# Layer 1's residual through VectorE block transposes and DRAM, and two groups' decay differences on ScalarE

## The chip, the cores and the metric

The kernel runs on one core of a Trainium2 chip. The metric is device time in microseconds (us), the median of several executions of the whole program. One more execution was taken with the hardware profiler; its times are the ones quoted from the profile.

## What is computed

Two layers work on 272 tokens (16 learned ones and 256 of the input) of width 2048, in float32. Layer 0 is linear attention beside stick-breaking attention. Layer 1, in which the change lies, is a Mamba-2 mixer (SSD). Each layer ends in `layer_norm(ALPHA * h + f(h))` with ALPHA = 4^(1/4). Cut to layer 1:

```python
proj = einsum('btd,de->bte', h, w_in)
z, xbc, dt_raw = split(proj)                    # 4096, 4096+2*1024, 64 columns
xbc = silu(causal_depthwise_conv(xbc, conv_w, conv_b))
xs, bs, cs = split(xbc)                         # 8 groups of 8 heads
dt = softplus(dt_raw + dt_bias)
a_cum = cumsum(dt * -exp(a_log))
l_mat = exp(where(causal, a_cum[t] - a_cum[s], -inf))   # the decay
y = einsum(l_mat * (cs . bs), xs * dt) + d_skip * xs    # the group's mixing
y = rms_norm_groups(y * silu(z), norm_w, 8)
h = layer_norm(ALPHA * h + y @ w_out, ln_g, ln_b)
```

## The kernel before

**Layout.** The hidden state is kept with channels on partitions: `hacc` is 16 tiles of 128 channels by 272 tokens. Layer 1's output is built the other way, with tokens on partitions: `acc` holds two tiles of 128 tokens by 2048 channels. The residual ALPHA·h has to come from the first form into the second, which is a transposition of 2048 x 256 numbers.

**Units.** The weights stream in as units of 1 MB (L144, on the queue of SyncE, SP; three buffers `raw`). ScalarE (ACT) rounds each half to `whi` (L159), VectorE (DVE) or GpSimd (POOL) forms the rest `wlo` (L160), and TensorE (PE) multiplies: three products per pair of tiles (L178 to L180), 48 matmuls per input unit of 128 output columns. Every float32 product is made so. A group of layer 1 has the input units B, C, four x and four z; from the second group on, output units (L494 to L496, then L503 adds into `acc`) come two groups behind their mixing. I write z1 and z2 for the second and third z unit of group 0.

**Side tasks.** All else runs as tasks that are stepped between the matmuls of the units. A scheduler with a model of the machine then sets the order on each engine, but no engine waits for another except by data, by a buffer that is not free yet, or because its instructions are in order.

**Layer 1's start (`first1`).** Six units (B, C, z0, x0, x1, x2 of group 0) are multiplied before the normalisation of layer 0 is applied. `fix` (L955 to L958) applies it to their results afterwards: a small copy, L956 and L957 on DVE, then ACT; L956 also frees the PSUM bank, of which the units share four. Meanwhile `normalize0` (L994 on DVE, L997 on ACT) normalises `hacc` itself. Then `xhi` (ACT, L981) and `xlo` (DVE, L982) are split from it, 16 pieces each, for all units that follow: the last x unit (x3), z1, z2 and so on.

**The residual (`residual1`).** 32 PE transposes (L1010) of 128 x 128 go into PSUM, and eight ACT copies (L1011) bring them to `acc`, multiplied by ALPHA.

**The decay.** `dt_path` forms dt and its cumulated sums, writes them to DRAM (edr, L1048) and transposes them with PE (L1055) into `est`. For each group `load_decay` reads edr back, broadcast to all partitions (ebc, L1092, 1664 KB), into the buffer that held `hacc`. `decay1` then forms, for each of the eight heads, min(ebc − est, 0) with two DVE instructions (L1125 with 256 columns, L1126 with 144), and an Exp on ACT for each two heads (L1128); after products with the causal part this is M, a single buffer.

**The mixing (`mix_ssd`).** PE multiplies M with x·dt (L1255, L1261), DVE adds the skip (L1265), POOL multiplies by the gate (L1266), ACT forms yh (L1268) and squares (L1271, L1274), POOL adds the squares up (L1275) into ysq, and PE sums them over the channels (L1281) for the group's RMS norm. The factor of that norm, `rstd1`, is applied when the output units' results are added to `acc`.

Of the kernel before, what the change touches and what calls it, by code (L numbers as in the profile page):

```python
# [6 lines left out]
F32 = mybir.dt.float32  # L7
F32R = mybir.dt.float32r
AF = mybir.ActivationFunctionType
# [79 lines left out]
class _Body:  # L89
# [413 lines left out]
            self.nc.vector.scalar_tensor_tensor(a, ps, r[:, t : t + 1], a, op0=ALU.mult, op1=ALU.add)  # L503

    def out1_unit(self, i, u, split_next):
        self.finish(*self.mixers[6 + u[1]])
        pst = [self.pj(), self.pj()]
        for h in range(2):
            split_next(h)
            for t in range(2):  # L510
                self.out1_half(pst[t], u[1], t, *self.parts[i, h], h)
                self.tick()
        for t in range(2):
            self.out1_add(pst[t], u[1], t, u[2])
# [428 lines left out]
    def first1(self):  # L943


        nc, lp = self.nc, self.lp
        act, vec = nc.scalar.activation, nc.vector
        b1 = len(L0)

        def fix(ps, n, t0, o=None):  # L950
            w = T - t0
            uv = lp.tile([P, 2], F32, tag="uv", name=self.nm("uv"), bufs=2)
            if o is None:
                o = lp.tile([P, T], F32, tag="yu", name=self.nm("fix"), bufs=2)
            vec.tensor_copy(uv[:n], ps[:n, w : w + 2])  # L955
            vec.scalar_tensor_tensor(o[:n, :w], mean[:n, t0:], uv[:n, 0:1], ps[:n, :w], op0=ALU.mult, op1=ALU.subtract)  # L956
            vec.tensor_tensor(o[:n, :w], o[:n, :w], self.rs_p[:n, t0:], op=ALU.mult)  # L957
            act(o[:n, :w], o[:n, :w], AF.Identity, bias=uv[:n, 1:2], scale=-1.0)  # L958
            return o

        scr = lp.tile([P, HPG, 400], F32, tag="M", name="dt_scr").rearrange("p a b -> p (a b)")
        mean = scr[:, 2048 + T : 2048 + 2 * T]
        act(mean, self.mean_p, AF.Copy)

        both = scr[:64, 2048 + 2 * T : 2048 + 2 * T + TG]
        act(both, self.ps_dt[64:128, :TG], AF.Copy)
        vec.tensor_tensor(both, both, self.ps_dt[:64, :TG], op=ALU.add)
        self.tasks["dt"] = self.push(self.dt_path(fix(both, 64, 0, scr[:, 2048 : 2048 + T]), scr))
        self.normed = False
        norm = self.push(self.normalize0())  # L970
        self.tasks["res"] = self.push(self.residual1(norm))
        for n, u in enumerate(L1[:NFIRST]):
            i = b1 + n
            self.load_unit(i + 2)
            ps = self.pj()
            t0 = {"z": NM, "C": C0}.get(u[2], 0)
            self.in_unit(ps[:, : TG - t0], i, t0, TG, lambda h: self.split_half(i + 1, h))
            self.post(u, fix(ps, P, t0))
        self.finish(norm)
        for k in range(KT):  # L980
            act(self.xhi[:, k, :T], self.hacc[:, k, :], AF.Copy)  # L981
            vec.tensor_tensor(self.xlo[:, k, :T], self.hacc[:, k, :], self.xhi[:, k, :T].bitcast(F32), op=ALU.subtract)  # L982
        self.normed = True
        self.last = [
            next(i for i in reversed(self.traced()) if i.engine == e)
            for e in (mybir.EngineType.Activation, mybir.EngineType.DVE)
        ]
# [12 lines left out]
    def residual1(self, norm):  # L1000

        nc = self.nc
        while not self.normed:
            yield
        for t in range(2):
            for c in range(4):
                ps = self.po()
                for k in range(4):
                    a = self.hacc[:, 4 * c + k, NM + t * P : NM + (t + 1) * P]
                    nc.tensor.transpose(ps[:, k * P : (k + 1) * P], a, self.ident)  # L1010
                nc.scalar.activation(self.acc[:, t, c * 512 : (c + 1) * 512], ps, AF.Copy, scale=ALPHA)  # L1011
                yield

    def dt_path(self, ps, scr):
# [72 lines left out]
            self.load_decay(g)  # L1087

    def load_decay(self, g):
        eb = self.hp.tile([P, HPG, 416], F32, tag="hacc", name=self.nm("ebc"))  # L1090
        src = self.edr[g * HPG : (g + 1) * HPG, :].rearrange("h c -> (h c)").partition_broadcast(P)
        self.nc.sync.dma_start(eb.rearrange("p h c -> p (h c)"), src)  # L1092
        self.cur["ebc", g] = eb
# [5 lines left out]
    def decay1(self, g):  # L1099
# [22 lines left out]
        eb = self.cur["ebc", g]  # L1122
        for h in range(HPG):
            gh = g * HPG + h
            vec.tensor_scalar(M[:, h, 0:256], eb[:, h, 0:256], self.est[:, 0, 0, gh : gh + 1], 0.0, op0=ALU.subtract, op1=ALU.min)  # L1125
            vec.tensor_scalar(M[:, h, 256:400], eb[:, h, 256:400], self.est[:, 0, 1, gh : gh + 1], 0.0, op0=ALU.subtract, op1=ALU.min)  # L1126
            if h % 2:
                act(M[:, h - 1 : h + 1, :], M[:, h - 1 : h + 1, :], AF.Exp)  # L1128
                yield
        mt = self.mt  # L1130
        e2 = self.est2[:, 0, g * HPG : (g + 1) * HPG].rearrange("p (h o) -> p h o", o=1).broadcast_to([16, HPG, 16])
# [104 lines left out]
    def mix_ssd(self, g):  # L1236
# [46 lines left out]
        tmp = lp.tile([P, 2], F32, tag="rt", name=self.nm("rt"))  # L1283
        r = lp.tile([P, 2], F32, tag="rr", name=self.nm("rr"), bufs=3)
        self.rstd1[g] = r
        vec.tensor_scalar(m, ps[:, 0:32:16], 1.0 / 512, RMS_EPS, op0=ALU.mult, op1=ALU.add)
        act(r, m, AF.Ln)
        act(r, r, AF.Exp, scale=-0.5)
        self.newton(r, m, tmp)
# [2 lines left out]
    def tail(self):  # L1292
# [51 lines left out]
        def moments(t):  # L1344
            v, r, _, _ = sc[t]
            vec.bn_aggr(mvs[t], sts[t])
            if t == 1:
                act(dm, nid, AF.Copy, scale=mvs[t][:, 0:1])
            vec.tensor_scalar(v, mvs[t][:, 1:2], LN_EPS, None, op0=ALU.add)
            act(r, v, AF.Ln)  # L1350
            act(r, r, AF.Exp, scale=-0.5)

# [126 lines left out]
```

## Time and profile before

| | |
|---|---|
| time, median of 3 runs | 1382.75 us (1382.08 to 1382.94) |
| span of the profiled execution | 1385.0 us |
| PE busy | 1374.1 us, 99% of the span |
| DVE busy | 1030.8 us, 74% |
| ACT busy | 768.3 us, 55% |
| POOL busy | 263.1 us, 19% |
| layer 1's 32 transposes on PE (L1010) | 710.8 to 733.0 us |
| group 0's decay differences on DVE | 769.3 to 774.1 us |
| the wait of PE for group 0's ysq | 804.4 to 806.4 us |

The span runs from the first to the last instruction of the one profiled execution; it lies 2.25 us above the median of the runs. In a timeline row the columns are the start, the time until the last of the row's instructions ends, engine, line and operation, the written tile and what it reads, the shape and the count; in brackets stands how long the engine was idle before, and who ended that. Matmuls overlap, so the distance from one start to the next is what one costs. Page rows of DMA give the count, the size of one and the median time from issue to landing.

### The profile page before, as it was taken

What the parts mean: (1) busy time and instruction counts of PE and PEld (TensorE: products, weight loads), DVE (VectorE), ACT (ScalarE), POOL (GpSimd) and SP (SyncE); (2) the same over time, 40 slices, a digit from 0 to 9 for tenths busy, and PEclk for the clock granted to TensorE, in tenths of its full rate; (3) what the DMA queues carried; (4) which work ended last, traced back from release to release, by engine and by line L of the source; (5) the groups of instructions that cost most, each with busy time, mean ns of one, the idle gap of its engine ahead of it and who ended that gap; (6) DMA issues with size and microseconds to landing.
All of it is one profiled execution on the core that took longest, in us unless ns stands there. A gap on an engine that the chain in (4) does not pass through costs nothing.

```text
span 1385.0 us, 26232 instructions
## 1 busy us (share of the span) xinstructions
PE 1374.1 (99%) x10643; PEld 1323.9 (96%) x10643; DVE 1030.8 (74%) x1762; ACT 768.3 (55%) x1141; POOL 263.1 (19%) x253
## 2 busy tenths in 40 slices
PE   9999999999999999999999999999999999999998
PEld 8999999999999999999999999899898999989986
DVE  7858576576565674568899999787877778867687
ACT  6646455355345544556587667656565655656551
POOL 0000100100101100004401143331322323133221
PEclk9999999999999999999999999999999999999999
DMA  9656446546455545554355655465555555455561
GB/s 329 209 172 201 163 163 206 169 155 227 153 173 171 169 161 191 172 165 161 123 183 197 231 181 205 169 244 182 209 177 195 190 191 222 169 198 183 181 214 61
DMA packets 61945, 256.73 MB, mean 185 GB/s; under 512 B 26176, under 2 KB 29056, under 8 KB 33408
## 3 DMA queue, kind: packets, MB, share of 16 engines
q1 hardware_dynamic: 61104, 254.27, 53.3%
q8 instruction: 83, 1.36, 0.4%
q10 hardware_dynamic: 720, 0.79, 0.2%
q14 instruction: 38, 0.31, 0.1%
HBM read 249.29 MB, written 5.74 MB: 184 GB/s over the span
## 4 chain that ended last, share of the span: by engine, by line
PE 94%; DVE 4%; DMA 1%; issue 1%; POOL 0%; ACT 0%; SPq 0%; ACTq 0%; DVEq 0%; POOLq 0%
PE pj L179 25%; PE pj L178 25%; PE pj L180 25%; PE pj L494 4%; PE pj L496 4%; PE pj L495 4%; PE po L1255 1%; PE po L631 1%; DVE wlo L160 1%; PE po L1193 0%; DMA raw<-in_wts 0%; DVE M L1125 0%; PE z L1143 0%; DVE xt L1070 0%; DVE acc L503 0%
## 5 line engine op out<-in xcount | busy, mean ns | idle before, releaser
L178 PE MATMUL pj<-xhi,whi 128*128 128x272 f32 (+4 forms) x2560 | 732.1, 286 | 1.7 <-ACT xhi L330 0.8
L179 PE MATMUL pj<-xlo,whi 128*128 128x272 f32 (+4 forms) x2560 | 730.8, 286 | 0.0
L180 PE MATMUL pj<-xhi,wlo 128*128 128x272 f32 (+4 forms) x2560 | 730.1, 286 | 0.0
L159 ACT ACTIVATE whi<-raw 128x1024 fp32r<-128x1024 f32 (+2 forms) x434 | 449.2, 1039 | 398.3 <-PE pj L179 326.3
L160 DVE TENSOR_TENSOR wlo<-raw,whi 128x1024 fp32r<-128x1024 f32 (+2 forms) x405 | 503.4, 1247 | 209.6 <-ACT whi L159 199.6
L178 PEld LDWEIGHTS pj<-xhi,whi 128*128 128x128 f32 x2560 | 482.6, 189 | 4.3 <-ACT whi L159 1.1
L179 PEld LDWEIGHTS pj<-xlo,whi 128*128 128x128 f32 x2560 | 482.6, 189 | 1.2 <-issue 0.6
L180 PEld LDWEIGHTS pj<-xhi,wlo 128*128 128x128 f32 x2560 | 482.6, 189 | 0.8 <-issue 0.8
L178 PE MATMUL pj<-mixh,whi 128*128 128x272 f32 x384 | 111.0, 290 | 0.0
L180 PE MATMUL pj<-mixh,wlo 128*128 128x272 f32 x384 | 110.7, 289 | 0.0
L179 PE MATMUL pj<-mixl,whi 128*128 128x272 f32 x384 | 110.7, 288 | 0.0
L160 POOL TENSOR_TENSOR wlo<-raw,whi 128x1024 fp32r<-128x1024 f32 x29 | 73.1, 2520 | 193.7 <-ACT whi L159 193.7
L494 PE MATMUL pj<-whi,yh 128*128 128x512 f32 (+1 forms) x240 | 93.3, 389 | 0.0
L495 PE MATMUL pj<-wlo,yh 128*128 128x512 f32 (+1 forms) x240 | 92.6, 386 | 0.0
L496 PE MATMUL pj<-whi,yl 128*128 128x512 f32 (+1 forms) x240 | 92.2, 386 | 0.0
L261 POOL TENSOR_TENSOR gr<-gr,gsc 128x1088 f32<-128x1088 f32 x6 | 15.4, 2574 | 303.6 <-ACT gsc L260 303.6
L179 PEld LDWEIGHTS pj<-mixl,whi 128*128 128x128 f32 x384 | 72.4, 188 | 0.2
L180 PEld LDWEIGHTS pj<-mixh,wlo 128*128 128x128 f32 x384 | 72.3, 188 | 0.0
L178 PEld LDWEIGHTS pj<-mixh,whi 128*128 128x128 f32 x384 | 72.2, 188 | 0.2
L503 DVE SCALAR_TENSOR_TENSOR acc<-pj,rr,acc 128x512 f32<-128x512 f32 (+1 forms) x65 | 46.5, 733 | 13.9 <-PE pj L496 13.9
L496 PEld LDWEIGHTS pj<-whi,yl 128*128 128x128 f32 x240 | 45.1, 188 | 9.2
L494 PEld LDWEIGHTS pj<-whi,yh 128*128 128x128 f32 x240 | 45.1, 188 | 8.9
(347 smaller groups left out, 1462.4 us busy)
## 6 DMA issues: line engine op xcount, KB each, us to landing
raw<-in_wts SPq DMA_DIRECT2D x212, 1024.0 KB, 4.8
ebc<-edr SPq DMA_DIRECT2D x8, 1664.0 KB, 6.4
raw<-in_wts SPq DMA_DIRECT2D x9, 256.0 KB, 6.3
vdr<-vt SPq DMA_DIRECT2D x8, 256.0 KB, 5.2
vt<-vdr SPq DMA_DIRECT2D x32, 64.0 KB, 2.4
hacc<-in_xT SPq DMA_DIRECT2D x7, 272.0 KB, 5.3
early<-in_wts SPq DMA_DIRECT2D x2, 512.0 KB, 7.7
vdr<-vt SPq DMA_DIRECT2D x8, 128.0 KB, 3.4
```

The costliest lines, as they stand in the source:

```text
L159: self.nc.scalar.activation(hi, src, AF.Copy)
L160: eng.tensor_tensor(lo, src, hi.bitcast(F32), op=ALU.subtract)
L178: mm(ps, whi, xhi, start=first, stop=False)
L179: mm(ps, whi, xlo, start=False, stop=False)
L180: mm(ps, wlo, xhi, start=False, stop=last)
L261: mul(c, c, e, op=ALU.mult)
L494: mm(ps, yh[:, kk, tt], hi[:, k, :], start=kk == 0, stop=False)
L495: mm(ps, yh[:, kk, tt], lo[:, k, :], start=False, stop=False)
L496: mm(ps, yl[:, kk, tt], hi[:, k, :], start=False, stop=kk == 3)
L503: self.nc.vector.scalar_tensor_tensor(a, ps, r[:, t : t + 1], a, op0=ALU.mult, op1=ALU.add)
L631: mm = lambda r, a, b, start=False, stop=False: self.nc.tensor.matmul(o[:, r], a, b, start=start, stop=stop, skip_group_check=True)
L1255: pin(mm(ov[p][i * 64 : (i + 1) * 64, jj, t0:S], xd[:, s, h * 64 : (h + 1) * 64], M[:, h, c0:c1], start=(s, jj) == (0, 0), stop=False, **gk,))
```

## The change

- `residual1` issues nothing any more; it only yields eight times.
- A new task, `residual_tokens`, is written so that it begins when group 0's mixer has been issued. In eight pieces (two token tiles, four blocks of 512 channels) it does: a DVE transpose of 128 x 512 (L1019), which transposes each block of 32 x 32 by itself, into `rst`, one buffer; a write of 256 KB to DRAM on SP (L1023); and four reads of 64 KB into `acc` on SP (L1026), in runs of 32 numbers, which put the blocks in their places. The output units wait for this task too.
- `acc` now holds h instead of ALPHA·h. In its place the RMS norm's constants get ALPHA², and the last layer norm's epsilon is divided by ALPHA².
- ebc has a buffer of its own instead of the one of `hacc`.
- For groups 0 and 1 the decay differences are ACT Relus of (est − ebc), and the Exp has a scale of −1; the other groups keep DVE.
- The program asks for a scratch of 128 for dynamic DMAs.

The lines behind L1003 move down by one and, later, by up to 20: L1070 is L1086 in the new kernel, L982 is L983, L1125 and L1126 are L1144 (ACT) and L1146 (DVE), L1255 is L1275, L1281 is L1301.

```diff
     def out1_unit(self, i, u, split_next):
-        self.finish(*self.mixers[6 + u[1]])
+        self.finish(*self.mixers[6 + u[1]], self.tasks["acc"])
...
         self.tasks["res"] = self.push(self.residual1(norm))
+        self.tasks["acc"] = self.push(self.residual_tokens())
...
         while not self.normed:
             yield
+        for _ in range(8):
+            yield
+
+    def residual_tokens(self):
+
+        nc = self.nc
+        while not self.mixers[6]:
+            yield
+        yield from _wait(*self.mixers[6])
         for t in range(2):
             for c in range(4):
-                ps = self.po()
-                for k in range(4):
-                    a = self.hacc[:, 4 * c + k, NM + t * P : NM + (t + 1) * P]
-                    nc.tensor.transpose(ps[:, k * P : (k + 1) * P], a, self.ident)
-                nc.scalar.activation(self.acc[:, t, c * 512 : (c + 1) * 512], ps, AF.Copy, scale=ALPHA)
+                st = self.hp.tile([P, 512], F32, tag="rst", name=self.nm("rst"))
+                src = self.hacc[:, 4 * c : 4 * c + 4, NM + t * P : NM + (t + 1) * P]
+                nc.vector.transpose(
+                    st.rearrange("p (k b x) -> p k b x", b=4, x=32), src.rearrange("p k (b x) -> p k b x", x=32)
+                )
+                d = self.tc.dram_tile([4, 32, 4, 4, 32], F32, name=self.nm("rdr"))
+                nc.sync.dma_start(d.rearrange("a i k b x -> (a i) (k b x)"), st)
+                o = self.acc[:, t, c * 512 : (c + 1) * 512].rearrange("q (k a x) -> q k a x", a=4, x=32)
+                for b in range(4):
+                    nc.sync.dma_start(o[32 * b : 32 * b + 32], d[:, :, :, b].rearrange("a i k x -> i k a x"))
+                yield
                 yield
...
-        eb = self.hp.tile([P, HPG, 416], F32, tag="hacc", name=self.nm("ebc"))
+        eb = self.hp.tile([P, HPG, 416], F32, tag="ebc", name=self.nm("ebc"))
...
-            vec.tensor_scalar(M[:, h, 0:256], eb[:, h, 0:256], self.est[:, 0, 0, gh : gh + 1], 0.0, op0=ALU.subtract, op1=ALU.min)
-            vec.tensor_scalar(M[:, h, 256:400], eb[:, h, 256:400], self.est[:, 0, 1, gh : gh + 1], 0.0, op0=ALU.subtract, op1=ALU.min)
+            for s, c in ((0, slice(0, 256)), (1, slice(256, 400))):
+                e = self.est[:, 0, s, gh : gh + 1]
+                if g < 2:
+                    act(M[:, h, c], eb[:, h, c], AF.Relu, bias=e, scale=-1.0)
+                else:
+                    vec.tensor_scalar(M[:, h, c], eb[:, h, c], e, 0.0, op0=ALU.subtract, op1=ALU.min)
             if h % 2:
-                act(M[:, h - 1 : h + 1, :], M[:, h - 1 : h + 1, :], AF.Exp)
+                act(M[:, h - 1 : h + 1, :], M[:, h - 1 : h + 1, :], AF.Exp, scale=-1.0 if g < 2 else 1.0)
...
-        vec.tensor_scalar(m, ps[:, 0:32:16], 1.0 / 512, RMS_EPS, op0=ALU.mult, op1=ALU.add)
+        vec.tensor_scalar(m, ps[:, 0:32:16], ALPHA ** 2 / 512, ALPHA ** 2 * RMS_EPS, op0=ALU.mult, op1=ALU.add)
...
-            vec.tensor_scalar(v, mvs[t][:, 1:2], LN_EPS, None, op0=ALU.add)
+            vec.tensor_scalar(v, mvs[t][:, 1:2], LN_EPS / ALPHA ** 2, None, op0=ALU.add)
```

The order on three engines shows where the new instructions stand. First DVE, where `xhi` has been split and x3 and z1 are about to be multiplied; `fix_8473` and `fix_8540` are the results of z0 and x0, and the second frees the PSUM bank that z1 takes. Before:

```order
L956 SCALAR_TENSOR_TENSOR fix_8473<-dt_scr,uv_8472,pj_8409 128x256
L982 TENSOR_TENSOR xlo<-hacc,xhi 128x272 x4
L957 TENSOR_TENSOR fix_8473<-fix_8473,z_65 128x256
L982 TENSOR_TENSOR xlo<-hacc,xhi 128x272 x3
L160 TENSOR_TENSOR wlo_8787<-raw_8620,whi_8786 128x1024
L982 TENSOR_TENSOR xlo<-hacc,xhi 128x272 x2
L1070 SCALAR_TENSOR_TENSOR bc_8321<-fix_8398,cpk,bc_8321 128x256
L982 TENSOR_TENSOR xlo<-hacc,xhi 128x272 x6
```

And now:

```order
L956 SCALAR_TENSOR_TENSOR fix_8473<-dt_scr,uv_8472,pj_8409 128x256
L1019 STREAM_TRANSPOSE rst_9641<-hacc 128x512
L983 TENSOR_TENSOR xlo<-hacc,xhi 128x272 x6
L957 TENSOR_TENSOR fix_8473<-fix_8473,z_65 128x256
L160 TENSOR_TENSOR wlo_8775<-raw_8620,whi_8774 128x1024
L983 TENSOR_TENSOR xlo<-hacc,xhi 128x272 x5
L1086 SCALAR_TENSOR_TENSOR bc_8321<-fix_8398,cpk,bc_8321 128x256
L983 TENSOR_TENSOR xlo<-hacc,xhi 128x272 x2
L1019 STREAM_TRANSPOSE rst_9682<-hacc 128x512
L983 TENSOR_TENSOR xlo<-hacc,xhi 128x272 x2
```

`rst_9641` and `rst_9682` are the third and fourth of the eight pieces: they stand among the xlo pieces, long before the mixing of group 0. The first two stand behind the normalisation, the other four up to the scans of `dt_path`.

Second, the SP queue at the same place; `raw_8620` is the weight unit of z1. Before, weight loads follow one another there:

```order
L144 DMA raw_8551<-in_wts 128x2048
L144 DMA raw_8620<-in_wts 128x2048
L144 DMA raw_8727<-in_wts 128x2048
L144 DMA raw_8841<-in_wts 128x2048
L144 DMA raw_8931<-in_wts 128x2048
```

And now:

```order
L144 DMA raw_8620<-in_wts 128x2048
L1023 DMA rdr_9540<-rst_9538 128x512
L144 DMA raw_8727<-in_wts 128x2048
L1026 DMA acc<-rdr_9540 32x16x32 x4
L1023 DMA rdr_9593<-rst_9591 128x512
L144 DMA raw_8817<-in_wts 128x2048
L1026 DMA acc<-rdr_9593 32x16x32 x4
L1023 DMA rdr_9643<-rst_9641 128x512
```

Each write stands behind the four reads of the piece before, with about one weight load between. It goes on so for eight pieces; the edr write and the first ebc read stand behind the last reads.

Third, PE at the sum of group 0's squares. Before, it stands in a z unit of group 1 (256 columns):

```order
L178 MATMUL pj_9759<-xhi,whi_9726 128x256
L179 MATMUL pj_9759<-xlo,whi_9726 128x256
L1281 MATMUL po_9540<-ones,ysq_9284 128x16 x2
L1193 MATMUL po_9777<-ident,xt_9353 128x128 x4
L180 MATMUL pj_9759<-xhi,wlo_9727 128x256
```

And now in the first unit of group 2 (B, 272 columns):

```order
L178 MATMUL pj_9929<-xhi,whi_9898 128x272
L179 MATMUL pj_9929<-xlo,whi_9898 128x272
L1301 MATMUL po_9492<-ones,ysq_9236 128x16 x2
L1213 MATMUL po_9777<-ident,xt_9305 128x128 x4
L180 MATMUL pj_9929<-xhi,wlo_9899 128x272
```

Between the last matmuls with M of group 0 and this step stood 151 matmuls of weight units (L178 to L180); now there are 189.

More of the change, by code (lines that the diff above doesn't have):

```diff
@@ L1467 @@
     names = ["xT", "wts", "wgu", "wdt", "wg2", "cpk", "dta", "lnr"]
-    nc = bacc.Bacc("TRN2", target_bir_lowering=False, num_devices=1)
+    nc = bacc.Bacc("TRN2", target_bir_lowering=False, num_devices=1, dynamic_dma_scratch_size=128)
     arrays, args = {}, []
```

## The prediction

> **What bounds the kernel now.** I read the page first: who is busy, and the chain that ended last.
>
> ```profile
> PE 1374.1 (99%) x10643; PEld 1323.9 (96%) x10643; DVE 1030.8 (74%) x1762; ACT 768.3 (55%) x1141; POOL 263.1 (19%) x253
> PE 94%; DVE 4%; DMA 1%; issue 1%; POOL 0%; ACT 0%; SPq 0%; ACTq 0%; DVEq 0%; POOLq 0%
> ```
>
> TensorE (PE) sets the time. So an edit is worth the PE work that it removes, plus or minus what it does to PE's few waits. I then read PE's timeline where layer 1 begins and where group 0's mixing ends.
>
> ```profile
> 725.52 1.14 PE L1010 MATMUL po<-ident,hacc 128*128 128x128 f32 x8 [0.37 <-ACT acc L1011]
> 727.11 0.38 PE L178 MATMUL pj<-xhi,whi 128*128 128x256 f32 x1 [0.46 <-DVE fix L956]
> ...
> 732.66 0.60 PE L1010 MATMUL po<-ident,hacc 128*128 128x128 f32 x4
> 733.02 0.37 PE L178 MATMUL pj<-xhi,whi 128*128 128x256 f32 x1
> ...
> 783.39 1.63 PE L1255 MATMUL po<-M,xd 128*64 128x256 f32 x20
> ...
> 806.41 0.62 PE L1281 MATMUL po<-ones,ysq 128*128 128x16 f32 x4 [2.06 <-POOL ysq L1275]
> ...
> 808.17 0.41 PE L179 MATMUL pj<-xlo,whi 128*128 128x256 f32 x1
> 808.38 0.41 PE L180 MATMUL pj<-xhi,wlo 128*128 128x256 f32 x1
> ...
> 810.57 0.29 PE L179 MATMUL pj<-xlo,whi 128*128 128x256 f32 x1
> 810.69 0.28 PE L180 MATMUL pj<-xhi,wlo 128*128 128x256 f32 x1
> ```
>
> The windows give each stretch its length, the busy time of PE, PE's loads, DVE, ACT and POOL, and PE's granted clock:
>
> ```profile
> 730.00:755.00 25.00, 25.00 (x213) 24.77 (x213) 23.88 (x47) 16.55 (x26) 3.01 (x3) 1.00 0.52 178
> ...
> 808.00:810.00 2.00, 2.00 (x11) 2.00 (x11) 1.95 (x8) 1.38 (x3) 0.00 (x0) 0.50 0.00 0
> ```
>
> Two places matter. At 727.11 the weight unit z1 starts, released by VectorE's (DVE's) L956; I call the matmul at 733.02 the start of z2. At 806.41 PE has waited 2.06 us for the squares of group 0 (ysq), and then matmuls start every 0.21 us instead of 0.12, up to about 810.3, at a granted clock of 0.50 (the windows' last row). So that wait costs 2.06 + about 1.9 (half of 3.8) = 3.9 us.
>
> **Part 1: 32 transposes leave PE.** Four of them take 733.02 − 732.66 = 0.36 us, so 32 are worth about 2.9 us. Eight stand in the hole before 727.11 that DVE ends, and so cost nothing; the other 24 are worth about 2.2. This is no gain of its own: z1 waits for DVE, and what counts is when DVE lets z1 go. The eight copies that leave ScalarE (ACT) also gain nothing here.
>
> **Part 2: eight block transposes join DVE.** The order puts them not behind the mixing of group 0 but from the normalisation on, in the stretch where DVE is full:
>
> ```profile
> 705.24 1.21 DVE L160 TENSOR_TENSOR wlo<-raw,whi 128x1024 fp32r<-128x1024 f32 x1
> ...
> 711.37 1.03 DVE L1070 SCALAR_TENSOR_TENSOR bc<-fix,cpk,bc 128x271 f32<-128x271 f32 x2 [1.98 <-ACT bc L1066]
> ...
> 715.07 0.47 DVE L956 SCALAR_TENSOR_TENSOR fix<-dt_scr,uv,pj 128x256 f32<-128x256 f32 x1
> 715.46 1.49 DVE L982 TENSOR_TENSOR xlo<-hacc,xhi 128x272 fp32r<-128x272 f32 x4
> 716.87 0.41 DVE L957 TENSOR_TENSOR fix<-fix,z 128x256 f32<-128x256 f32 x1
> 717.20 1.14 DVE L982 TENSOR_TENSOR xlo<-hacc,xhi 128x272 fp32r<-128x272 f32 x3
> 718.26 1.22 DVE L160 TENSOR_TENSOR wlo<-raw,whi 128x1024 fp32r<-128x1024 f32 x1
> 719.40 0.79 DVE L982 TENSOR_TENSOR xlo<-hacc,xhi 128x272 fp32r<-128x272 f32 x2
> 720.10 0.48 DVE L1070 SCALAR_TENSOR_TENSOR bc<-fix,cpk,bc 128x256 f32<-128x256 f32 x1
> 720.50 2.20 DVE L982 TENSOR_TENSOR xlo<-hacc,xhi 128x272 fp32r<-128x272 f32 x6
> ...
> 726.58 0.48 DVE L956 SCALAR_TENSOR_TENSOR fix<-dt_scr,uv,pj 128x272 f32<-128x272 f32 x1
> ```
>
> A block transpose of layer 0 (minimum, median and maximum in ns), two of its writes on the SP queue with the reads that wait for them, and the page's median landing of such a write:
>
> ```profile
> L586 DVE STREAM_TRANSPOSE vt<-pj x24: 395/449/451, 25.3 to 624.2; 128x256 f32<-128x256 f32 x24
> 99.10 0.33 SPq L600 DMA_DIRECT2D vdr<-vt  x1
> ...
> 103.37 2.53 SPq L604 DMA_DIRECT2D vt<-vdr  x4
> ...
> 201.28 0.33 SPq L600 DMA_DIRECT2D vdr<-vt  x1
> ...
> 205.97 2.53 SPq L604 DMA_DIRECT2D vt<-vdr  x4
> vdr<-vt SPq DMA_DIRECT2D x8, 256.0 KB, 5.2
> ```
>
> From the starts: an xlo piece takes 0.35 us, L957 0.33, a wlo split 1.14, a conv step (L1070) 0.40. The nearest transpose is half as wide and takes 0.40 to 0.45; I estimate 0.7 for 512 columns (0.6 to 0.9). The buffer rst is single: transpose n+1 waits until write n has landed. On the SP queue write n+1 stands behind four reads, which also wait for write n. Layer 0's writes of the same size were followed by their reads after 4.27 and 4.69 us, and the four reads held the queue for 2.53. I take 4.6; the page's median of 5.2 is the upper end.
>
> Transpose 1 stands at 705.24 and ends at about 705.95. Write 1 lands at 710.55; transpose 2 fits into the idle 1.98 us before 711.37. Write 2 goes out at 710.55 + 2.53 = 713.1 and lands at 717.7. Transpose 3 stands behind L956 and one xlo piece, at 715.46 + 0.35 = 715.8 by the row: DVE waits 1.9. From there to the end of the L956 that frees z1, the order has two transposes (1.4), 15 xlo pieces (5.3), three splits (3.4), two conv steps (0.8), L957 (0.3), small ones (an estimate of 0.5) and L956 itself (0.48): 12.2 us. z1 starts at 729.9, which is 2.8 later than now. Meanwhile PE has little to do: without its 24 transposes it would reach z1 near 723, and unit x3 now ends with the last xlo, at about 726.3 by the same sum. It then stands idle for 3.6 us. A shorter idle time, 2.06 us, brought the half clock at 806, so I take the 1.9 us again. z1 lasts 5.5 (48 matmuls of 0.114); z2 starts at 729.9 + 5.5 + 1.9 = 737.3 against 733.02: **+4.3**.
>
> [...]
>
> Ends of this term: with writes that land in 3.6 us transpose 3 does not wait, and at the full clock z2 starts at 715.8 + 12.2 + 5.5 = 733.5 (+0.5). Below that it can't go, because L956 at 726.58 already sets z1 and two transposes stand ahead of it. With 5.2, transpose 3 starts at 718.9, transpose 4 waits for write 3 another 0.6, and z2 starts at 739.1 (+6.1).
>
> The other five transposes add 3.5 us to a DVE that is busy for 23.88 of 25 us from 730 to 755, but PE itself is 4.3 later there, so what DVE hands to it has 0.8 more cover than now; I take nothing.
>
> **Part 3: the decay of group 0.** The edr write and the ebc read now stand on SP behind the eighth piece.
>
> ```profile
> 755.12 0.50 SPq L1048 DMA_DIRECT2D edr<-dt_scr  x1
> ...
> 757.33 1.51 SPq L1092 DMA_DIRECT2D ebc<-edr  x1
> ebc<-edr SPq DMA_DIRECT2D x8, 1664.0 KB, 6.4
> ```
>
> A difference on DVE, a row of like size on ACT, and what ACT and POOL do on the way to ysq:
>
> ```profile
> L1125 DVE TENSOR_SCALAR M<-ebc,est x64: 334/343/2557, 769.3 to 1235.4; 128x256 f32<-128x256 f32 x64
> L1274 ACT ACTIVATE ys<-yu x24: 400/402/404, 794.4 to 1335.7; 128x256 f32<-128x256 f32 x24
> 790.98 1.04 ACT L159 ACTIVATE whi<-raw 128x1024 fp32r<-128x1024 f32 x1
> ...
> 792.57 0.86 ACT L1128 ACTIVATE M<-M 128x800 f32<-128x800 f32 x1
> 793.34 0.49 ACT L1268 ACTIVATE yh<-yu,cpk 128x256 fp32r<-128x256 f32 x1
> ...
> 804.20 2.15 POOL L1275 TENSOR_TENSOR ysq<-ysq,ys 128x256 f32<-128x256 f32 x2
> ```
>
> Eight writes and seven groups of reads with a weight load between: 705.95 + 8 × 4.6 + 7 × 2.86 = 762.8; the last reads and one load, and edr goes out at 765.6, 10.5 later than now. ebc follows 2.2 later and lands after 6.4, at 774.2. Sixteen Relus of at most 0.40 each (L1274 is the like-sized ACT row) make 6.4, and four Exps of 0.86 with a split of 1.04 after each the rest: the last Exp ends near 787.2. PE's last reads of M, now at 783.39, come 4.3 + 3.5 later (29 more matmuls stand ahead in the order, the removed transposes counted out): 791.2. So about 4 us of cover are left. Bounds: 0 with the cover, up to 2 with 5.2 us per write (edr 4.8 later still); I take **+0.4** for the transposes of est, whose scans are late by DVE's load.
>
> **Part 4: the squares of group 0.** From the mixing's end (783.39 + 1.63 = 785.0) to the end of the last POOL sum (806.35) the chain lasts 21.3 us. In the order 151 weight matmuls stand between the two PE steps before, 189 now: 38 × 0.12 = 4.5 us more cover, against a wait of 2.06. On ACT group 1's Relus come first: 6.4, a split 1.04 and two Exps 1.7 put yh 9.1 us behind the mixing, where it was 8.3 (793.34): 0.8 lost. The wait goes with 1.6 to spare, and the half clock with it: **−3.9** (0 if the chain grows by over 1.6 us and the clock falls again). DVE loses 32 L1125/L1126 for groups 0 and 1 (16 × 0.34 and 16 shorter ones), about 10 us in all, but behind 769, where no PE wait but this one hangs on it. The constants, the smaller DMA scratch and ebc's own tile cost nothing: no row of a step changes by them.
>
> Sum: +4.3 + 0.4 − 3.9 = +0.8 on the profiled execution's 1385.0 (span). The median is 1382.75, 2.25 below that span; I apply the sum to the median: 1383.5.
>
> **Rivals.**
> A, faster: the writes land in about 3.9 us and the clock stays full. Transpose 3 then starts at 716.3, z1 at 728.5, z2 at 734.0: +1.0 − 3.9 = −2.9, 1379.9. For it: 4.27 was measured with traffic around. Against: idle PE lost its clock at 806. Chance 0.13.
> B, slower: each write takes over 5 us, because weight loads and the 128-byte reads share the queues. Z2 +6.1, est and M +1.5, −3.9: +3.7 at 5.2, and another 1.5 for each further 0.5; around 1387. The page's 5.2 speaks for it. It decides from about 5 us. Chance 0.20.
> C, slower: ACT, in order, holds yh behind the Relus of group 1, which wait for PE's last read of the single M. If they take over 1.6 us more than summed, the wait on ysq and the half clock come back: +4.7, 1387.4. For it: POOL's steps stretch under DVE load. Chance 0.19.
> D: the change does not do what it says, since its pieces run ahead of the mixing; that is in every sum above.
>
> [...]
>
> **How the numbers follow.** A measurement of this kernel can tell about 0.2%, 2.8 us, from no change: faster means below 1380.0, slower above 1385.5. Forecast 0.43 (+0.8, own range 1381.5 to 1385.5), A 0.13, B 0.20, C 0.19, unknown 0.05. Faster: A and a bit, 0.14. Slower: B and C, less their mild ends, 0.37. Same: 0.49. The range from 1379.5 to 1388.0 leaves out the far ends of B and C.
>
> **What would show it.** Right: no L1010 on PE; z1 after 729, released by L956, with a clock near 0.5 behind it; DVE waits for a DMA before its third transpose; no ysq wait on PE. Wrong: z1 before 728.5 (the writes are quicker), a PE wait on M or est near 780, or a PE wait on ysq of over 1 us.

## The result and the profile after

The changed kernel takes 1399.1 us (median of 4 runs, 1398.63 to 1400.42), the kernel before 1382.85 in the same session (4 runs, 1382.08 to 1385.17): ratio 1.0118, 95% interval 1.0107 to 1.0130. It is 16.3 us slower, far outside the predicted range. The profiled execution of after took 1398.63, with a span of 1396.9.

The page of after, its busy times and its chain:

```profile
PE 1376.1 (99%) x10611; PEld 1325.4 (95%) x10611; DVE 1029.2 (74%) x1738; ACT 774.4 (55%) x1165; POOL 261.3 (19%) x253
PE 42%; DVE 3%; DMA 1%; ACT 1%; POOL 1%; issue 1%; SPq 0%; ACTq 0%; POOLq 0%
```

PE has 32 instructions fewer and is busy 2 us longer: a share of them ran at a slower clock, granted at 0.50 as shown below. "99%" hides 16 us, since the damage is local. It shows in PE's waits of the stretch from 690 to 870 us of after (waiting tile and line, releaser, then us in total, times, longest):

```profile
PE pj L178 <- ACT gz L1242: 5.4, 1, 5.4
PE pj L178 <- DVE fix L956: 3.2, 1, 3.2
PE po L1071 <- DVE dt_scr L1062: 2.5, 1, 2.5
PE pj L179 <- DVE xlo L983: 1.3, 2, 1.0
PE po L1301 <- POOL ysq L1295: 0.6, 1, 0.6
```

The same waits in a second profile of the kernel before (run e5 below, span 1380.3):

```profile
PE pj L178 <- DVE fix L956: 0.5, 1, 0.5
PE po L1010 <- ACT acc L1011: 0.4, 1, 0.4
PE po L1281 <- POOL ysq L1275: 0.2, 1, 0.2
```

13.0 us of waits against 1.1. The rest is the clock. The trace records the clock that was granted to PE as stretches with a start and a length. In after, between 690 and 870 us, three stretches at 0.50 stand: 725.66 to 732.49, 766.62 to 770.04 and 821.24 to 828.06, that is 6.8, 3.4 and 6.8 us. Windows of after cut at those borders (PE's busy time and matmuls stand behind the length; the granted clock is the third number from the end):

```profile
722.25:725.66 3.41, 2.04 (x13) 1.47 (x11) 3.41 (x10) 1.92 (x4) 0.00 (x0) 1.00 0.95 283
725.66:729.08 3.42, 1.30 (x6) 1.33 (x7) 3.42 (x6) 0.39 (x1) 0.00 (x0) 0.50 0.68 177
729.08:732.49 3.41, 3.41 (x18) 3.41 (x18) 3.41 (x7) 0.00 (x0) 0.00 (x0) 0.50 0.62 96
732.49:735.90 3.41, 3.41 (x32) 3.41 (x32) 3.10 (x7) 3.02 (x5) 0.00 (x0) 1.00 1.01 324
...
763.21:766.62 3.41, 0.87 (x7) 0.56 (x7) 3.41 (x9) 3.41 (x6) 0.00 (x0) 1.00 0.98 364
766.62:770.04 3.42, 3.42 (x18) 3.22 (x16) 3.42 (x8) 2.29 (x4) 1.05 (x1) 0.50 0.82 167
...
817.82:821.24 3.42, 0.00 (x0) 0.00 (x0) 3.30 (x4) 0.00 (x0) 3.42 (x1) 1.00 0.70 252
821.24:824.65 3.41, 2.48 (x11) 2.48 (x12) 1.61 (x3) 2.91 (x8) 1.89 (x3) 0.50 0.93 320
824.65:828.06 3.41, 3.41 (x17) 3.41 (x17) 1.23 (x1) 0.38 (x2) 0.00 (x0) 0.50 0.16 67
```

In these rows a slice that PE fills holds 32 matmuls at full clock and 17 or 18 at half. From the granted 0.50 I take half of PE's busy time in a half-clock slice as its cost, an estimate: (1.30 + 3.41 + 3.42 + 2.48 + 3.41) / 2 = 7.0 us. So the waits (13.0 − 1.1) and the clock (7.0), less the 2.9 of the removed transposes, make 16.0 us. The spans differ by 1396.9 − 1380.3 = 16.6.

PE's timeline of after, at the places that the prediction speaks of:

```profile
727.78 0.55 PE L178 MATMUL pj<-xhi,whi 128*128 128x256 f32 x1 [3.16 <-DVE fix L956]
...
765.87 0.27 PE L1071 MATMUL po<-ident,dt_scr 64*128 64x64 f32 x1 [2.54 <-DVE dt_scr L1062]
...
796.00 1.63 PE L1275 MATMUL po<-M,xd 128*64 128x256 f32 x20
...
822.17 0.59 PE L178 MATMUL pj<-xhi,whi 128*128 128x272 f32 x1 [5.39 <-ACT gz L1242]
```

And the last mixing of group 0 in the second profile of before:

```profile
782.16 1.63 PE L1255 MATMUL po<-M,xd 128*64 128x256 f32 x20
```

The mixing of group 0 ends at 797.6 instead of 783.8. The largest wait, at 822.17, is one that the prediction never names: a weight matmul that finds no free PSUM bank, since ACT's gate evictions of group 1 (L1242) stand still. ACT and POOL of after show for what:

```profile
797.68 5.75 ACT L1144 ACTIVATE M<-ebc,est 128x256 f32<-128x256 f32 x16 [0.38 <-PE po L1275]
...
821.74 0.94 ACT L1242 ACTIVATE gz<-pj 128x256 f32<-128x256 f32 x3 [5.31 <-POOL yu L1286]
```

```profile
801.32 1.43 POOL L1286 TENSOR_TENSOR yu<-yu,gz 128x256 f32<-128x256 f32 x2 [22.42 <-DVE yu L1285]
807.85 1.39 POOL L1286 TENSOR_TENSOR yu<-yu,gz 128x256 f32<-128x256 f32 x1
814.46 7.24 POOL L1286 TENSOR_TENSOR yu<-yu,gz 128x256 f32<-128x256 f32 x1 [3.77 <-DVE yu L1285]
```

gz has one buffer. Group 1's gates can't be written until POOL has read group 0's fourth gate, at 814.46 + 7.24 = 821.70. POOL of the second profile of before:

```profile
797.33 1.01 POOL L1266 TENSOR_TENSOR yu<-yu,gz 128x256 f32<-128x256 f32 x1 [0.32 <-POOL yu L1266]
```

There it is done at 798.3, so gz comes free 23.4 us later in after. Of that, 13.8 are the later end of the mixing. Another 3.6 lie between that end and the fourth skip add on DVE, which hands the product its input (813.84 − 797.6 = 16.2 in after, 796.42 − 783.8 = 12.6 in the second profile of before):

```profile
813.84 0.48 DVE L1285 SCALAR_TENSOR_TENSOR yu<-xt,cpk,po 128x256 f32<-128x256 f32 x1
```

Nearly all of the last 6.0 is the product itself, 7.24 us long instead of 1.01.

### The profile page after: what moved, and what is told of

The parts are those of the page before. It is cut to its first block, busy times and chain, and to the rows that moved or that the text cites. A ratio compares the mean times of both kernels' runs of the same rounds, so it can differ in the third digit from the quotient of the medians.

```text
span 1396.9 us, 26229 instructions
## 1 busy us (share of the span) xinstructions
PE 1376.1 (99%) x10611; PEld 1325.4 (95%) x10611; DVE 1029.2 (74%) x1738; ACT 774.4 (55%) x1165; POOL 261.3 (19%) x253
## 5 line engine op out<-in xcount | busy, mean ns | idle before, releaser
L178 PE MATMUL pj<-xhi,whi 128*128 128x272 f32 (+4 forms) x2560 | 734.0, 287 | 9.4 <-ACT gz L1242 5.4
L180 PE MATMUL pj<-xhi,wlo 128*128 128x272 f32 (+4 forms) x2560 | 732.2, 286 | 0.0
L178 PEld LDWEIGHTS pj<-xhi,whi 128*128 128x128 f32 x2560 | 484.9, 190 | 11.5 <-ACT gz L1242 5.6
L180 PEld LDWEIGHTS pj<-xhi,wlo 128*128 128x128 f32 x2560 | 484.6, 189 | 1.3 <-issue 1.2
L178 PE MATMUL pj<-mixh,whi 128*128 128x272 f32 x384 | 111.0, 290 | 0.0
L180 PE MATMUL pj<-mixh,wlo 128*128 128x272 f32 x384 | 110.7, 289 | 0.0
L180 PEld LDWEIGHTS pj<-mixh,wlo 128*128 128x128 f32 x384 | 72.3, 188 | 0.0
L178 PEld LDWEIGHTS pj<-mixh,whi 128*128 128x128 f32 x384 | 72.2, 188 | 0.2
L503 DVE SCALAR_TENSOR_TENSOR acc<-pj,rr,acc 128x512 f32<-128x512 f32 (+1 forms) x65 | 46.5, 733 | 13.8 <-PE pj L496 13.8
```

The costliest lines, as they stand in the source:

```text
L178: mm(ps, whi, xhi, start=first, stop=False)
L180: mm(ps, wlo, xhi, start=False, stop=last)
```

## The experiments

The theories on which the expectations below speak: Q, the residual's new path (DVE's eight transposes, one rst buffer, the SP queue) makes DVE late and PE pays for it; R, the Relus on ACT, in order, hold back what follows the mixing of group 0. When the first runs were in, the single gz, the half clock and POOL's long product were set against each other. All ratios are against the kernel before, on the same chip, with 95% intervals. "PE waits" are those from 690 to 870 us. The scheduler sets the order anew for every edit, so two runs can differ by more than the edit; where that matters, the text says so.

**e1, the residual alone.** Everything of the change but the Relus:

```diff
-                if g < 2:
+                if g < 0:
...
-                act(..., AF.Exp, scale=-1.0 if g < 2 else 1.0)
+                act(..., AF.Exp, scale=1.0)
```

> The residual's part alone: the decay differences of all groups stay on DVE, everything else as in the changed kernel. Theory Q (the pieces' round trips through DRAM hold DVE and SP, and all the lateness follows from there): z1 2.9 us late, a PE wait for est of 2 to 3 us near 763, and group 0's mixing as late as in the changed kernel, so the wait on gz near 816 stays: 1394 to 1400 us. Theory R (the wait on gz comes from group 1's Relus, which stand ahead of yh on ScalarE): the first two losses stay, the wait on gz goes: 1388 to 1392 us.

Measured: 1391.2 us, ratio 1.0060 (1.0045 to 1.0075), +9.0. PE waits 3.2 at z1, 2.6 at est, 1.0 on xlo, 0.3 on ysq; half clock 4.8 us. The gz wait is gone: POOL's fourth product ends at 817.3 and group 1's gates start there. That is what R expected, in the time and in the waits; Q had the gz wait stay. So the residual alone costs 9 of the 16.

**e2, the decay alone.** The kernel before with the Relus and the negated Exp for groups 0 and 1:

```diff
...
+                if g < 2:
+                    act(M[:, h, c], eb[:, h, c], AF.Relu, bias=e, scale=-1.0)
...
```

> The decay's part alone on the kernel before: 32 Relus of groups 0 and 1 on ScalarE, the residual by PE transposes as before. Theory Q: ScalarE has room, DVE gets 10 us back, no wait of PE is added: 1381 to 1385 us. Theory R: yh stands about 6 us later behind group 1's Relus, and PE waits 4 to 6 us for gz or ysq, with a half clock behind it: 1388 to 1392 us.

Measured: 1382.16 us (10 runs), ratio 0.9999 (0.9989 to 1.0008). PE waits 0.5 and 0.4, clock full. The Relus by themselves cost nothing and gain nothing, which is what Q expected and not R. Zero and 9.0 don't make 16.3: the two halves of the change interact, and neither theory had that.

**e3, seven rst buffers** (ebc shares its tile again, to have the room):

```diff
-                st = self.hp.tile([P, 512], F32, tag="rst", name=self.nm("rst"))
+                st = self.hp.tile([P, 512], F32, tag="rst", name=self.nm("rst"), bufs=7)
...
-        eb = self.hp.tile([P, HPG, 416], F32, tag="ebc", name=self.nm("ebc"))
+        eb = self.hp.tile([P, HPG, 416], F32, tag="hacc", name=self.nm("ebc"))
```

> The changed kernel with seven rst buffers instead of one (ebc shares hacc's buffer again, as before, to make room). No transpose then waits for a write to land. Theory Q: the eight transposes cost DVE only their 0.7 us each, z1 is late by at most 5 us since all stand ahead of it, but the 7 us of DVE waits and the wait for est go, and the mixing comes earlier; gz is not waited for: 1384 to 1390 us. Theory R: only the wait for est goes (4 us), the wait on gz stays: 1393 to 1396 us.

Measured: 1388.99 us, ratio 1.0050 (1.0033 to 1.0066). The size was in reach of Q, the way was not. PE has one long wait left:

```profile
PE pj L178 <- DVE fix L956: 9.9, 1, 9.9
```

With buffers free, the order puts all eight transposes ahead of the L956 that frees z1 (the last five run together from 709.92). est and gz then wait for nothing: edr goes out at 750.2, against 768.04 in after. The single buffer spreads the delay over three places; without it all of it lies at one, and costs less in total.

**e4, two gz buffers:**

```diff
-            self.cur["z", g] = self.lp.tile([P, 4, S], F32, tag="gz", name=self.nm("gz"))
+            self.cur["z", g] = self.lp.tile([P, 4, S], F32, tag="gz", name=self.nm("gz"), bufs=2)
```

(and the same on the other tile of that tag, with ebc's tile as in e3.)

> The changed kernel with two gz buffers instead of one (ebc shares hacc's buffer again to make room). Group 1's gates then need not wait for POOL's last read of group 0's. If the single gz buffer is what PE waits for near 816, that wait goes with the half clock behind it, 5 to 9 us: 1390 to 1394 us. If POOL's late product is what counts whatever the buffers, PE waits at the sum of the squares instead: 1396 to 1400 us.

Measured: 1390.07 us, ratio 1.0056 (1.0041 to 1.0071), 7.9 us over the kernel before instead of 16.3, as the reading by the single gz had it. POOL and ACT of e4:

```profile
812.96 7.59 POOL L1286 TENSOR_TENSOR yu<-yu,gz 128x256 f32<-128x256 f32 x1 [3.76 <-DVE yu L1285]
```

```profile
802.53 0.36 ACT L1242 ACTIVATE gz<-pj 128x256 f32<-128x256 f32 x1
810.10 0.37 ACT L1242 ACTIVATE gz<-pj 128x256 f32<-128x256 f32 x1
```

POOL's product is as long as in after, and no gate eviction waits for it. That the gz wait goes is the second buffer's doing; ebc's return to its old tile was not run by itself, so a part of the 8 us could be its. What is left is of the size of e1's loss: waits of 3.2, 1.9, 1.4 and 1.4 us.

**e5, the kernel before, unchanged, a second profile.**

> The kernel before, unchanged, for a second profile. If the wait of 2.06 us for ysq with the half clock behind it belongs to every execution, this profile shows it again near 804, and the span is near 1385. If it belonged to the first profiled execution alone, PE has no such wait and the span is about 3.5 to 4 us shorter, near 1381: then the 3.9 us that the forecast took off the median were never in the median.

Measured: 1382.03 us, clock 1.000, and the wait on ysq is 0.2 us instead of 2.06. The execution on which the prediction was worked out had a wait that the typical one doesn't have. It may not be the only one: of the 40 runs of the kernel before that were timed with the experiments three, of 1385.47 to 1386.86 us, have its mean granted clock of 0.998, and all others 0.999 or 1.000. In the execution with the wait POOL works without a gap from 798.40 to the end of the last sum, and its last two gate products take 5.21 us, where e5 has 0.75 and 1.01 for the same two instructions:

```profile
798.40 5.21 POOL L1266 TENSOR_TENSOR yu<-yu,gz 128x256 f32<-128x256 f32 x2 [1.61 <-DVE yu L1265]
```

**e6, the transposes late.** Each of the eight is issued behind the last DVE instruction that was traced when group 0's mixing was done:

```diff
+        last = next(i for i in reversed(self.traced()) if i.engine == mybir.EngineType.DVE)
...
+                with self.tc.issue_after(last):
+                    nc.vector.transpose(
```

> The changed kernel with the eight transposes made to follow the mixing of group 0, as the change's words have it. Theory Q: DVE and SP are free for dt_path again, no wait for est, z1 no later than before, and no wait on gz: 1380 to 1384 us. Theory R: ScalarE's Relus still hold yh and so gz: PE waits 4 us or more near 816, 1387 to 1391 us.

Measured: 1391.14 us, ratio 1.0063 (1.0048 to 1.0078). Both theories missed: PE waits no more for est or gz, yet 8.5 us are lost. z1 still waits 3.1 us, though no transpose stands ahead of it, and group 1's squares are 4.2 us late. In that later stretch the weight loads stand on the SP queue behind the reads of the residual, which wait for the writes. That this makes the squares late is argued, and wasn't tried by itself.

**e7, late, and the decay on DVE** (e6 with the edit of e1):

> As the run with late transposes, with the decay differences of all groups on DVE. Theory Q: DVE has some 10 us more to do between 769 and 793 and eight transposes after that; the first is hidden, the second may meet the weight splits: 1380 to 1385 us. Theory R: 1380 to 1383 us, faster than the late run with Relus by 4 us or more.

Measured: 1388.63 us, ratio 1.0042 (1.0027 to 1.0057), slower than both theories had it. The same two waits, 3.1 at z1 and 2.7 on ysq. Against e6 it is 2.5 us faster, but the two intervals overlap.

**e8, Relus for group 0 only:**

```diff
-                if g < 2:
+                if g < 1:
...
-                act(..., AF.Exp, scale=-1.0 if g < 2 else 1.0)
+                act(..., AF.Exp, scale=-1.0 if g < 1 else 1.0)
```

> The changed kernel with Relus for group 0 only; group 1's differences are on DVE. z1 and est are late as in the changed kernel. If group 1's Relus, which stand ahead of yh on ScalarE, make the wait on gz, it goes: 1389 to 1392 us, as with the residual alone. If group 0's Relus make it, because they finish M later than DVE did, it stays: 1396 to 1400 us.

Measured: 1400.18 us, ratio 1.0127 (1.0110 to 1.0144). PE's longest wait grows:

```profile
PE pj L178 <- ACT gz L1242: 7.8, 1, 7.8
```

So the gz wait needs no Relus of group 1 on ACT. Group 0's are enough: e8 differs from e1 in them alone, and is 9.0 us slower. The run doesn't clear group 1's differences altogether, since on DVE they now stand ahead of the last two skip adds (814.30 and 818.76). Rival C, as the prediction put it, falls by the trace of after: yh starts at 805.81, 8.2 us behind the mixing as before, and PE waits 0.6 for ysq.

**e9, late, with PE's transposes back.** e6 and the 32 PE transposes into PSUM that nobody reads:

```diff
-        for _ in range(8):
-            yield
+        for t in range(2):
+            for c in range(4):
+                ps = self.po()
+                for k in range(4):
+                    a = self.hacc[:, 4 * c + k, NM + t * P : NM + (t + 1) * P]
+                    nc.tensor.transpose(ps[:, k * P : (k + 1) * P], a, self.ident)
+                yield
```

> The late run again, with the 32 PE transposes of the kernel before added back, into PSUM that nobody reads: PE does their work for nothing. Theory C (what z1 loses in the late run is the clock: PE stands idle for over 3 us where eight transposes stood, and then runs at half speed): z2 starts where it does in the kernel before, about 2 us sooner than in the late run, although PE has 2.9 us more to do, and the whole is 0 to 3 us faster than the late run. If the idle time costs no clock: 2 to 3 us slower than the late run.

Measured: 1388.12 us, ratio 1.0040 (1.0025 to 1.0055), 3.0 less than e6 in another session; the two intervals overlap. z1 in PE's timeline, of e6 and of e9:

```profile
726.16 0.36 PE L178 MATMUL pj<-xhi,whi 128*128 128x256 f32 x1 [3.12 <-DVE fix L956]
```

```profile
726.51 0.39 PE L178 MATMUL pj<-xhi,whi 128*128 128x256 f32 x1 [0.62 <-DVE fix L956]
```

A slice of the windows behind it, of e6 and of e9:

```profile
726.86:730.28 3.42, 3.42 (x19) 3.42 (x18) 3.42 (x6) 0.18 (x1) 0.00 (x0) 0.50 0.69 280
```

```profile
728.23:731.64 3.41, 3.41 (x31) 3.41 (x30) 3.41 (x7) 2.31 (x4) 0.00 (x0) 1.00 0.43 178
```

z1 waits for DVE either way. The transposes stood in a hole that DVE ends, and their work there kept the clock: from z1 to the start of z2 PE takes 5.76 us instead of 7.26. By the profiles' times z2 starts 1.15 us sooner (732.27 against 733.42), not 2. Even that is mostly the start: e9 begins the normalisation 0.8 us sooner (698.04 against 698.84), and counted from there its z1 is 1.15 later and its z2 only 0.35 sooner; why z1 is later isn't shown. So the clock is shown, and that it makes the 3.0 us is not. The two profiled executions, 1391.86 and 1390.80 us, differ by only 1.1, and e9's is the longest of its four. In it, 6.4 us over the kernel before lie in the ysq wait of group 1 (3.6) and the half clock after it (2.8).

**e10, the changed kernel with PE's transposes back**, unread (the edit of e9 on after):

> The changed kernel with the 32 PE transposes added back, into PSUM that nobody reads. Theory C: no half clock behind z1, so PE reaches the est step at least 1 us sooner, and waits there longer, because DVE's scans end it: the whole is within 2 us of the changed kernel, 1397 to 1400. If PE's clock at z1 were what counts to the end: 1396 to 1397.5. If PE's own work counts there: 1401 to 1402.

Measured: 1390.23 us, ratio 1.0053 (1.0038 to 1.0068). All theories missed: with 32 matmuls whose output nobody reads the changed kernel is 9 us faster. No slice from 690 to 870 us runs at half clock, and from z1 to z2 PE takes 5.57 us instead of 7.73. The gz wait is gone, and there the order differs: the fourth skip add on DVE stands ahead of the products of M with the C·B term (M·cb), where after has it behind three of them (at 813.84), and POOL's product follows at 807.60 and takes 0.74 us.

```profile
806.51 0.48 DVE L1290 SCALAR_TENSOR_TENSOR yu<-xt,cpk,po 128x256 f32<-128x256 f32 x1
```

How much of the 9 us is the clock and how much the order, this run can't tell.

**e11, no transposes on DVE.** The writes take hacc as it lies, and the rst tile is gone; the blocks are not transposed, so acc holds numbers in a wrong order:

```diff
-                nc.sync.dma_start(d.rearrange("a i k b x -> (a i) (k b x)"), st)
+                nc.sync.dma_start(d.rearrange("a i k b x -> (a i) k (b x)"), src)
```

> The changed kernel without the eight block transposes: each write to DRAM takes its 256 KB from hacc directly, so acc gets numbers in a wrong order; all 40 transfers stay. Theory Q-DVE (DVE's 5 us of transposes and 7 us of waits make the scans and with them est and M late): no wait for est, mixing early, no wait on gz, z1 no later than before but for the half clock: 1382 to 1387 us. Theory Q-SP (the queue makes edr, ebc and weight loads late): the wait for est goes, the mixing stays late and the wait on gz too: 1391 to 1396 us.

Measured: 1387.54 us (10 runs), ratio 1.0023 (1.0011 to 1.0035), single runs from 1383.83 to 1389.61. z1 waits 3.1 and est 3.1: in this order PE comes to est at 753.1, where it came at 755.94 in e5, and the scans on DVE start at 755.47 (752.73 in e5). So the wait for est stays, which neither theory had, but the mixing ends at 788.2 (797.6 in after) and PE doesn't wait for gz, as Q-DVE said. The medians differ by 4.6 us and the ratio makes it 3.2: with the transposes and their waits off DVE, some 12 or 13 of the 16.3 are back.

**e12, group 0's gate product on DVE instead of POOL:**

```diff
-            nc.gpsimd.tensor_tensor(u, u, z[:, j, :], op=ALU.mult)
+            (nc.gpsimd if g else vec).tensor_tensor(u, u, z[:, j, :], op=ALU.mult)
```

> The changed kernel with group 0's four gate products (yu times gz) on DVE instead of POOL; the order of the rest moves by few rows. If the wait on gz near 816 comes from the chain over POOL, whose fourth product lasted 7.2 us beside a busy DVE, the wait and the half clock behind it go or shrink to under 1.5 us: 1389 to 1393 us. If it comes from ScalarE's Relus ahead of yh or from the late mixing whatever engine gates, the wait stays at 4 us or more: 1396 to 1400 us.

Measured: 1396.03 us, ratio 1.0095 (1.0078 to 1.0112). The gz wait shrinks from 5.4 to 1.3, as the first theory had it, but the time is that of the second: waits of 1.8 on M and 2.8 on ysq appear. With the products gone, POOL is slow at the next thing it does beside DVE, which is busy without a gap from 815.55 to 825.79; its two sums of squares take 10.53 us, the first of them at least 8.67 (817.13 to 825.80):

```profile
817.13 10.53 POOL L1295 TENSOR_TENSOR ysq<-ysq,ys 128x256 f32<-128x256 f32 x2 [6.35 <-ACT ys L1294]
```

So the run moves the delay and doesn't price it; that the whole chain behind the mixing is late, and POOL's 7 us only a part of it, is argued.

No version beats the kernel before; e2 is its equal. Not tried: several rst buffers with the transposes held at their places, the residual's pieces on a queue other than SP's, and the same order on all engines with only one thing changed.

## Why the prediction was wrong, step by step

**What bounds the kernel: right.** PE sets the time, and 16.0 of the 16.6 us of loss are PE's waits and the clock behind them.

**Part 4, the −3.9: void.** The wait on ysq and its half clock were in the one profiled execution and not in the median (e5: 0.2 us). e2, with the Relus alone, shows that there was nothing to win: ratio 0.9999. The span of an execution is 1.7 us shorter than its time (e5: 1380.3 and 1382.03; 1.67 to 1.79 in all runs of the experiments), so the one of 1385.0 lay about 4.0 us above the median, not 2.25. That is the whole of the 3.9: to work the sum out on it and then apply it to the median took a gain that the median had already.

**Part 1, "no gain of their own": right as far as it goes.** The step saw the transposes of the hole as free and the other 24 as useless to remove. It is Part 2 that priced the hole they leave, with 1.9 us of half clock. e6 and e9 part the two: without the PE transposes z1 waits 3.1 us also where no DVE transpose is near, and with them back (e9) z1 runs at the full clock, 1.5 us shorter. How much of that reaches the end isn't shown.

**Part 2, +4.3: the direction and most of the size right.** The sum had z1 2.8 later and z2 4.3. In after z1 starts at 727.78 and z2 at 735.51, 1.9 and 3.7 later than in e5 (725.88 and 731.79), and 0.7 and 2.5 later than in the first profile of before, which was itself 1.2 behind e5 there. The half clock behind z1 cost (1.30 + 3.41) / 2 = 2.4 where 1.9 was taken. 0.7 us per transpose was right:

```profile
L1019 DVE STREAM_TRANSPOSE rst<-hacc 128x512 f32<-128x512 f32 x8 | 5.6, 705 | 7.2 <-DMA rdr<-rst 7.2
```

But the waits before z1 were small, 0.20 where 1.9 was taken, and the later ones long. DVE of after:

```profile
715.59 0.71 DVE L1019 STREAM_TRANSPOSE rst<-hacc 128x512 f32<-128x512 f32 x1 [0.20 <-DMA rdr<-rst]
...
739.04 0.71 DVE L1019 STREAM_TRANSPOSE rst<-hacc 128x512 f32<-128x512 f32 x1 [3.45 <-DMA rdr<-rst]
747.92 0.71 DVE L1019 STREAM_TRANSPOSE rst<-hacc 128x512 f32<-128x512 f32 x1 [2.35 <-DMA rdr<-rst]
756.17 0.71 DVE L1019 STREAM_TRANSPOSE rst<-hacc 128x512 f32<-128x512 f32 x1 [1.18 <-DMA rdr<-rst]
...
765.10 1.15 DVE L1062 TENSOR_TENSOR_SCAN dt_scr<-dt_scr 64x272 f32<-64x272 f32 x3
```

**Part 2's last sentence, "the other five transposes … I take nothing", and Part 3's +0.4: the first failed steps.** The sum put the waits on rst before z1 and none behind it. They came behind: 3.45 + 2.35 + 1.18 = 7.0 us in front of transposes 6 to 8, and DVE, in order, kept everything behind them. (Four transposes stand behind z1, not five, as the order has it: 2.8 us of work.) The landing of the eight writes of after (minimum, median, maximum):

```profile
DMA to landing us min/median/max: 2.0/4.5/7.2
```

SP's queue around the slowest of them:

```profile
729.80 0.58 SPq L144 DMA_DIRECT2D raw<-in_wts  x1
...
731.80 0.63 SPq L1023 DMA_DIRECT2D rdr<-rst  x1
739.03 2.60 SPq L1026 DMA_DIRECT2D acc<-rdr  x4
```

The median of 4.5 is the 4.6 that was taken. The spread did the harm: the fifth write went out 2 us after a weight load of 1 MB and landed after 7.2. That the load made it slow is not shown; the sixth, 0.7 us behind a load, landed after 5.5. So rival A was right that the third transpose hardly waits and wrong about the clock. Rival B was right that writes can take over 5 us (three of the eight did), but priced what follows at z1 for the most part, with 1.5 for est and M. The scans that est needs start at 765.10, where the first profile of before has

```profile
753.95 1.14 DVE L1046 TENSOR_TENSOR_SCAN dt_scr<-dt_scr 64x272 f32<-64x272 f32 x3
```

and PE waited 2.5 us for them, plus 1.7 of half clock: 4.2 instead of 0.4. The "0.8 more cover" was PE's own lateness (4.3) less the added work (3.5), and it left the waits out. DVE was busy for 23.88 of 25 us before, and the added work moved what stands behind it by its whole length, its waits included: the scans start 11.2 us later, and 9.8 of that are the four transposes and their waits.

**Part 4's chain and rival C: the failed step that cost most.** The chain from the mixing was followed to one consumer, the squares. Its cover was nearly long enough: PE waited 0.6 us for ysq in after, where the gz wait had held it up before, and 1.4 in e4, where that wait is gone. The same chain has a second consumer: POOL's product is the last reader of gz, gz is single, and the next gates fill PSUM banks that PE needs. That branch wasn't walked. It took 5.4 us of wait and 2.9 of clock, and in e4, with one more buffer, the wait is gone (7.9 us over the kernel before instead of 16.3).

**Why both halves together cost more.** In e1 group 0's mixing ends at 795.0 and POOL is done with gz at 817.3, and PE doesn't wait. In after they end at 797.6 and 821.7. Those 4.4 us turn a hidden wait into 5.4. Of them 2.7 are in the mixing: the Relus of group 0 stand between a late ebc and the products with M (e8 shows that group 0's are enough). In e2 the same Relus make the mixing 2.7 later too (786.5 against 783.8 in e5), but there it has its cover, and costs nothing. The other 1.8 lie behind the mixing: the fourth skip add comes 3.7 sooner after it than in e1 (16.2 against 19.9), but from that skip add to the end of POOL's product it is 7.9 us instead of 2.4.

**The signs named beforehand.** Right: no L1010, z1 released by L956 with a clock of 0.5 behind it, DVE waiting for a DMA before its third transpose (0.20), no ysq wait over 1 us. Of the three signs of "wrong" two came: z1 before 728.5 (727.78) and a PE wait on M or est, though at 765.87 (est) and not near 780. The gz wait was on no list.

## What to carry to other kernels

When a step at the bottleneck's edge gets later, walk to every reader that gives a buffer back, single buffers first, and not only to the result that the bottleneck waits for today. Price a wait of the matmul engine with its clock behind it, here 1.7 us for each filled slice of 3.4 us at half clock, and look at whether cheap matmuls in a hole were what kept the clock (from z1 to z2 5.76 us with them in e9, 7.26 without in e6). And profile the kernel twice before a wait seen once goes into a sum: its time must stand in the median's execution too, and span must be compared with span.

## What the runs showed of the hardware

**The granted clock changed on a grid of 3.41 us.** Eleven of the fourteen profiles show half clock between 690 and 870 us. Each such stretch is 3.4, 6.8 or 10.2 us long, and the stretches of an execution lie on one grid of 3.41 us, also with waits between them: in after 766.62 and 821.24 are 12 and 28 steps behind 725.66. Looked at by that grid, in the same 180 us, a slice at full clock in which PE was busy for 1.49 us or less was followed by half clock 19 times in 19; between 1.7 and 2.1 us, 2 times in 10; above 2.2, never. The first profile of before, around its ysq wait:

```profile
803.52:806.93 3.41, 1.35 (x13) 1.16 (x12) 2.81 (x2) 3.41 (x8) 2.76 (x6) 1.00 0.69 276
806.93:810.35 3.42, 3.42 (x18) 3.42 (x18) 3.37 (x10) 2.79 (x5) 0.00 (x0) 0.50 0.02 5
```

Here a wait of 2.06 us lay within one slice, and the next one ran at half clock. A wait of 2.4 us on est in e10 fell on a border, and cost no clock:

```profile
759.76:763.17 3.41, 1.96 (x16) 1.74 (x15) 3.41 (x7) 1.66 (x3) 0.00 (x0) 1.00 0.66 114
763.17:766.58 3.41, 2.45 (x20) 2.18 (x21) 3.41 (x8) 3.41 (x6) 0.00 (x0) 1.00 0.90 339
```

A slice need not be idle for half clock to follow: in the one from 803.52 PE was busy for 1.35 of 3.41 us, 40%.

**A product on POOL took 0.7 us or 7.2.** The 128x256 product took 0.74 us in the first profile of before, from 1316.71, while DVE was idle, and 7.24 in after, where it runs from 814.46 beside a DVE that multiplies and splits for 6.66 us of that time. The windows of both (DVE's busy time is the third number behind the length, POOL's the fifth):

```profile
1316.71:1317.45 0.74, 0.74 (x5) 0.61 (x4) 0.00 (x0) 0.67 (x2) 0.74 (x2) 1.00 0.90 376
```

```profile
814.46:821.70 7.24, 2.32 (x21) 2.12 (x19) 6.66 (x9) 1.97 (x3) 7.24 (x2) 0.97 0.80 281
```

A busy DVE doesn't always do it. Of the 64 such products in the first profile of before and in that of after 49 ran while DVE was busy for at least 95% of the time, and took 0.73 to 1.73 us; the only two of the 64 that took longer, 4.52 and 7.24, had DVE busy for 87% and 92%. The four beside an idle DVE took under 0.75, so that "POOL's steps stretch under DVE load" (rival C) is true of some of them only. In e10, where POOL's product (807.60) and DVE's M·cb products (807.52) start together, the one on POOL took 0.74 us. What makes the difference isn't shown, since no run here varied the DVE work alone.
